# A two-layer hybrid mixer/SwiGLU block: the FFN's opening order, its first down products, and a 4 + 2 split of the last output half

## The chip, the cores and the metric

The kernel runs on one core of one Trainium2 chip. The metric is the device time of one execution in microseconds (us), from the profiler; the engines are TensorE (PE), VectorE (DVE), ScalarE (ACT), GpSimd (POOL) and the queue from which nearly all transfers are issued, SyncE (SP).

## The reference, cut to what matters

Two layers over 512 latent and 256 context tokens of width 1024. A layer is a mixing sub-layer (three head groups, one projection in and one out) and a SwiGLU feed-forward network (FFN), each between two RMS norms with a modulation (shift, scale, gate) that is computed from conditioning vectors. The second layer keeps only the latent tokens after the mixer.

```python
def swiglu(h, w13, w2):              # h: tokens x 1024, FFN_HIDDEN = 2816
    gate, up = jnp.split(h @ w13, 2, axis=-1)
    return (jax.nn.silu(gate) * up) @ w2
...
mod_l = (jax.nn.silu(c) @ ada_w[l] + ada_b[l])[:, None, :]
...
h_l = modulate(rms_norm(lat, norm_ffn_pre[l]), sh2, sc2)
lat = lat + gt2 * rms_norm(swiglu(h_l, ffn_w13[l], ffn_w2[l]), norm_ffn_post[l])
```

Everything is float32.

## The kernel before, in words

**Precision.** A float32 operand of a product is split into a high and a low part of a faster type: ACT casts the high part, DVE or POOL subtracts to get the low part, and three PE products (high-high, high-low, low-high) are summed. So weights cost one ACT cast (`L328`) and one DVE subtraction (`L329`) for each buffer of 128x1024. `wp` holds one raw buffer and four `whi`/`wlo` buffers of this size; `load` and `load13` fill them, and `get(i, ahead=1)` loads one unit ahead in program order.

**Order.** The program is written in one order; a scheduler with a timing model then fixes each engine's order, program order being the priority. Pools are stacks in on-chip memory, on the left and on the right; a tile of a new pool waits for the old tiles that lay where it lies.

**End of the mixer.** For each block of 128 tokens (position `pos`; the order is context blocks 4, 5, then 0 to 3) `out_front` computes the output projection from four units `wos`, two of them in `wp`, two in a right pool; `out_back` of the block before does `post_norm` and `pre_norm`, which ends in PE transposes into `whole` (`L266`, then DVE `L274` and ACT `L272`). Then the rest of the modulation chunks (`ada_some`, products at `L203`) and the FFN.

**FFN up.** A Strassen-Winograd form: `whole` is cut in k (first index) and in token halves (`hn` = 384 columns in layer 0, 256 in layer 1) into b11, b12, b21, b22; DVE makes t1 to t4 from them, and b11, b21, b22, t1 to t4 are split. `thi` and `tlo` take the two buffers of tag `H`; `tlo` lies where `whole` was. For each of 22 hidden blocks f, `ffn_up` takes seven products of 12 matmuls (`prod`, `L1211`): a11 b11, s2 t2, s3 t3, s1 t1, a12 b21, a22 t4, s4 b22. Of the weight combinations POOL makes s3 and s1 (`L367`, `L368`), DVE s2 and s4 (`L369`, `L370`). The hidden block goes to DRAM (`hds`).

**FFN down.** For each half j of the output's 1024 columns, all 2816 hidden rows are read back in pairs of blocks (`hid_pair`: one transfer `hr`, two ACT casts `L1261`, one subtraction on DVE and one on POOL `L1262`) and multiplied with w2 (`down`, `L1270`, 6 matmuls of 512 columns for each pair and position), accumulating one bank for each position: six in layer 0, four in layer 1. w2 comes in groups of 2, 4, 4, 4, 4, 4 blocks. Half 0 is copied to `y0`. In the last group of half 1 the positions end one after another, and `ffn_back` (post-norm, residual, and in layer 0 the pre-norm of layer 1) follows one position behind.

**Pools that matter.** `adp` (constants `cst2` and modulation buffers `araw`, `arow`) lives through the kernel. The FFN's pool `F` (left) is opened after the mixer's pools `rx`, `mx` are closed, and the pool `D` of the down part lies where `F` lay.

Of the kernel before, what the change touches and what calls it, by code (L numbers as in the profile page):

```python
# [11 lines left out]
F32 = mybir.dt.float32  # L12
# [11 lines left out]
NL = 2  # L24
# [59 lines left out]
def tile_backbone(ctx: ExitStack, tc: tile.TileContext, a: dict, out: bass.AP, dbg=None):  # L84
# [274 lines left out]
    def load13(i, srcs):  # L359
        F = state["F"]  # L360
        raw = wtile(wp if i % 2 else F, "raw", [128, 4, 512])
        for dsl, src in srcs:
            DMA.dma_start(raw[:, dsl].rearrange("p s (k n) -> p (s k) n", n=128), src)
        a21, a22, a11, a12 = (raw[:, q] for q in range(4))
        sm = pt(F, "S", [128, 3, 512], bufs=1)
        s2, s3, s4 = (sm[:, q] for q in range(3))
        G.tensor_tensor(s3, a11, a21, ALU.subtract)  # L367
        G.tensor_tensor(a21, a21, a22, ALU.add)  # L368
        V.tensor_tensor(s2, a21, a11, ALU.subtract)  # L369
        V.tensor_tensor(s4, a12, s2, ALU.subtract)  # L370
        t0 = split(wp, raw[:, 2:4], [128, 2, 512], V)
        t1 = split(wp, sm[:, 0:2], [128, 2, 512], V)
        t2 = split(wp, raw[:, 0:2], [128, 2, 512], V)
        t3 = split(wp, sm[:, 2:3], [128, 1, 512], V)
        at = {"a11": (t0, 0), "a12": (t0, 1), "s2": (t1, 0), "s3": (t1, 1), "s1": (t2, 0), "a22": (t2, 1),
              "s4": (t3, 0)}
        return {n: tuple(t[q][:, o].rearrange("p (k n) -> p k n", n=128) for q in range(2))
                for n, (t, o) in at.items()}
# [17 lines left out]
    for l in range(NL):  # L396
# [18 lines left out]

        for f in range(NF):
            u["w13"][f] = add("w13", None,
                              [(slice(0, 2), kblk(w13[:, FF + 128 * f:FF + 128 * f + 128])),
                               (slice(2, 4), kblk(w13[:, 128 * f:128 * f + 128]))])
        for j in range(2):  # L420
            f0 = 0
            for gi, gn in enumerate(GROUPS):
                u["w2"][gi, j] = add("w2", [128, gn, 512],
                                     [((allsl,), kblk(a["ffn_w2"][l, 128 * f0:128 * (f0 + gn),
                                                                  512 * j:512 * j + 512]))])
                f0 += gn
# [65 lines left out]
    adp = ctx.enter_context(tc.tile_pool(name="adp", bufs=2))  # L492
    cst.append(pt(adp, "cst2", [128, CST.shape[1] - NC0], bufs=1))
    S.dma_start(cst[1], a["cst"][:, NC0:])
    ones = C("ones")
    tri = C("tri", "p (a f) -> p a f", a=2)
    gam = C("gam", "p (h f) -> p h f", h=4)
    qgf = C("qgf", "p (r f) -> p r f", r=2)
    qgb = C("qgb", "p (r f) -> p r f", r=2)
    kgf, kgb, rdec, hsel = C("kgf"), C("kgb"), C("rdec"), C("hsel")  # L500
    cosc = C("cos", "p (t f) -> p t f", t=4)
    sinc = C("sin", "p (t f) -> p t f", t=4)

# [6 lines left out]
    for l in range(NL):  # L510
# [6 lines left out]
        tbs_out = [0, 1, 2, 3] if last else tbs_all  # L517
        mx = ctx.enter_context(ExitStack())
# [647 lines left out]
        out_back(*prev)  # L1166
        rx.close()
        mx.close()

        ada_some(adp, len(todo))  # L1170

        hn = tot // 2
        with pool(f"F{l}") as F:
            state["F"] = F
            bhi = pt(F, "bhi", [128, 3, 4, hn], F32R, bufs=1)
            blo = pt(F, "blo", [128, 3, 4, hn], F32R, bufs=1)
            tm = pt(F, "tm", [128, 4, 4, hn], bufs=1)
            thi = pt(hp, "H", [128, 4, 4, hn], F32R)
            b11, b12 = whole[:, 0:4, 0:hn], whole[:, 0:4, hn:tot]
            b21, b22 = whole[:, 4:8, 0:hn], whole[:, 4:8, hn:tot]  # L1180
# [162 lines left out]
```

## Time and profile before

| what | value |
|---|---|
| median of 3 runs | 1896.7 us (1896.48 to 1901.89) |
| the profiled execution, its own time | 1899.01 us |
| its span, first to last instruction | 1897.1 us |
| mean granted TensorE clock | 0.963 of full speed |
| PE busy | 1768.9 us (93%) |
| HBM read, written | 226.82 MB, 36.31 MB |

The profiled execution is one of the same program; 1.9 us of its time lie outside the span. Busy times are sums over instructions; a PE that is busy can run at either of two clocks, 2.4 or 1.2 GHz, and the granted clock of a stretch is given as a share of the higher.

### The profile page before, as it was taken

Reading aid. Unit: us, or ns where it says so; the run is one execution under the profiler, and the core shown is the slowest. Engines: PE = TensorE matmul, PEld = TensorE weight load, DVE = VectorE, ACT = ScalarE, POOL = GpSimd, SP = SyncE. Lnnn points to the kernel's source line nnn. Section 1 sums busy time; section 2 is a strip of 40 time slices with the busy share of each in tenths; the row PEclk is TensorE's granted clock in tenths of the full one; section 3 lists DMA queues with packets and bytes.
Section 4 is the critical chain, followed back from the end, with each engine's and each line's share of the span. In section 5 each row is a group of like instructions: output and inputs, shape, how many; then the busy total and the mean of one; then the engine's idle time right before and its main releaser. Section 6 shows DMA issues by size and latency. Waiting matters only on the chain. (4 is left out here: it accounts for less than half of the span.)

```text
span 1897.1 us, 30528 instructions
## 1 busy us (share of the span) xinstructions
PE 1768.9 (93%) x11915; PEld 1581.0 (83%) x11915; DVE 1172.1 (62%) x2022; ACT 804.7 (42%) x1462; POOL 587.1 (31%) x569
## 2 busy tenths in 40 slices
PE   6999989998969999998999979999998879999898
PEld 4789988877958999998788747998887879999686
DVE  4677688746457565654434357659856488887345
ACT  3546443224553333333323375544334454444333
POOL 1103453204114332331412140145303135555322
PEclk9999999999979999999999989999998979999899
DMA  8334344547432333332645373334434234443753
GB/s 280 118 99 129 109 153 148 158 148 232 151 111 84 109 106 92 92 110 97 246 139 180 112 230 106 95 114 153 143 128 148 78 101 132 126 133 106 281 188 124
DMA packets 261259, 265.10 MB, mean 140 GB/s; under 512 B 13432, under 2 KB 220252, under 8 KB 260988
## 3 DMA queue, kind: packets, MB, share of 16 engines
q1 hardware_dynamic: 260048, 261.86, 43.2%
q8 instruction: 93, 1.52, 0.3%
q10 hardware_dynamic: 1068, 1.31, 0.2%
q14 instruction: 50, 0.41, 0.1%
HBM read 226.82 MB, written 36.31 MB: 139 GB/s over the span
## 5 line engine op out<-in xcount | busy, mean ns | idle before, releaser
L329 DVE TENSOR_TENSOR wlo<-raw,whi 128x1024 fp32r<-128x1024 f32 (+2 forms) x192 | 274.7, 1435 | 163.5 <-ACT whi L328 163.2
L1211 PE MATMUL px<-H,whi 128*128 128x384 f32 (+1 forms) x1408 | 310.9, 312 | 5.7 <-ACT whi L328 5.7
L328 ACT CAST whi<-raw 128x1024 fp32r<-128x1024 f32 (+2 forms) x192 | 194.4, 1018 | 241.1 <-PE px L1211 107.5
L433 PE MATMUL mm<-whi,H 128*128 128x256 f32 x1376 | 269.0, 290 | 7.1 <-ACT stg L793 6.4
L1211 PEld LDWEIGHTS px<-H,whi 128*128 128x128 f32 x1408 | 237.3, 191 | 7.4 <-ACT whi L328 7.4
L433 PEld LDWEIGHTS mm<-whi,H 128*128 128x128 f32 x1376 | 219.4, 192 | 21.8 <-ACT stg L793 9.1
L1211 PE MATMUL px<-H,wlo 128*128 128x384 f32 (+1 forms) x704 | 213.9, 311 | 0.0
L433 PE MATMUL mm<-wlo,H 128*128 128x256 f32 x688 | 198.4, 288 | 0.0
L433 PE MATMUL mm<-H,whi 128*128 128x256 f32 (+2 forms) x720 | 179.6, 338 | 5.5 <-DVE H L490 2.6
L1270 PE MATMUL px<-whi,hidhi 128*128 128x512 f32 x374 | 149.5, 401 | 15.8 <-ACT hidhi L1261 15.8
L1270 PE MATMUL px<-wlo,hidhi 128*128 128x512 f32 x374 | 149.5, 400 | 0.0
L1270 PE MATMUL px<-whi,hidlo 128*128 128x512 f32 x374 | 145.9, 395 | 0.0
L433 PEld LDWEIGHTS mm<-H,whi 128*128 128x128 f32 (+1 forms) x720 | 122.1, 189 | 28.0 <-DVE H L490 3.7
L328 ACT CAST whi<-S 128x1024 fp32r<-128x1024 f32 x88 | 73.6, 836 | 164.3 <-DVE S L369 69.6
L1262 POOL TENSOR_TENSOR hidlo<-hr,hidhi 128x768 fp32r<-128x768 f32 (+1 forms) x44 | 76.6, 1743 | 204.0 <-ACT hidhi L1261 191.5
L433 PEld LDWEIGHTS mm<-wlo,H 128*128 128x128 f32 x688 | 132.4, 192 | 2.4 <-issue 1.3
L1211 PEld LDWEIGHTS px<-H,wlo 128*128 128x128 f32 x704 | 132.4, 191 | 0.0
L1240 POOL TENSOR_TENSOR hf<-hf,g 128x384 f32<-128x384 f32 (+1 forms) x44 | 54.1, 1229 | 241.4 <-issue 174.6
L1211 PE MATMUL mm<-bhi,whi 128*128 128x384 f32 (+1 forms) x352 | 111.2, 316 | 14.2 <-ACT whi L328 14.2
L433 PE MATMUL px<-whi,H 128*128 128x256 f32 x640 | 120.8, 288 | 0.4 <-ACT H L1143 0.4
L433 PE MATMUL mm<-H,wlo 128*128 128x256 f32 (+2 forms) x360 | 120.0, 334 | 0.4 <-DVE wlo L329 0.4
L329 DVE TENSOR_TENSOR wlo<-S,whi 128x1024 fp32r<-128x1024 f32 x88 | 89.2, 1013 | 47.0 <-ACT whi L328 46.8
(304 smaller groups left out, 3920.5 us busy)
## 6 DMA issues: line engine op xcount, KB each, us to landing
araw<-ada_w_dram SPq DMA_DIRECT2D x96, 512.0 KB
raw<-ffn_w_dram SPq DMA_DIRECT2D x92, 512.0 KB
raw<-w_in_dram SPq DMA_DIRECT2D x26, 1024.0 KB
raw<-ffn_w_dram SPq DMA_DIRECT2D x20, 1024.0 KB
hr<-hd SPq DMA_DIRECT2D x22, 768.0 KB
hr<-hd SPq DMA_DIRECT2D x22, 512.0 KB
Rt<-gd SPq DMA_DIRECT2D x40, 256.0 KB
hd<-hf SPq DMA_DIRECT2D x22, 384.0 KB
```

Of the source, the lines that this page charges most:

```text
L328: S.copy(hi, src)
L329: lo_engine.tensor_tensor(lo, src, hi.bitcast(F32), ALU.subtract)
L433: PE.matmul(ps, x(k), y(k), start=(k == 0 and p == 0), stop=(k == n - 1 and p == 2))
L1211: PE.matmul(ps[:, :hn], w[x][:, k], r[y][:, k], start=first and k == 0 and p == 0, stop=k == 3 and p == 2, skip_group_check=True)
L1240: G.tensor_tensor(h1, h1, g1, ALU.mult)
L1262: (G if q else V).tensor_tensor(hh[1][:, q], hr[:, q], hh[0][:, q].bitcast(F32), ALU.subtract)
L1270: PE.matmul(ps, lh[x](k), rh[y](k), start=f + k == 0 and p == 0, stop=f + k == NF - 1 and p == 2, skip_group_check=True)
```

## The change

1. **Opening.** `load13` can load a unit of the gate columns only (`gate_only`: a11 and a12, one split). For the first NA hidden blocks (3 in layer 0, 4 in layer 1) such units are loaded first, and their products a11 b11 and a12 b21 open the FFN; the same blocks' other five products follow in `ffn_up`, whose units fetch all four quarters again but don't split a11 and a12 again (`late`). The splits and combinations of `whole` are made in column blocks of 128 tokens; b21's and b22's low parts and t3 go from DVE to POOL. `bhi`, `blo`, `tm` lie in a right pool `FB`.
2. **Down opening.** At f = 9 the hidden pairs 0 and 2 are read back and split into the place of `tm`; their down products stand ahead of the change from pool `F` to pool `D`.
3. **Passes.** In layer 0 the second column half is done in two passes, four positions and then two, each reading all hidden blocks and its own copy of w2's half. Layer 1 keeps two passes of four.
4. **Pools.** `adp` becomes a pool of each layer, closed before the FFN; layer 1 loads `cst2` again, on ACT's queue. The rest of `ada_some` moves ahead of the pools' closing. The raw buffers of `load13` alternate by f, odd f in `F`.

```diff
-        raw = wtile(wp if i % 2 else F, "raw", [128, 4, 512])
-        for dsl, src in srcs:
-            DMA.dma_start(raw[:, dsl].rearrange("p s (k n) -> p (s k) n", n=128), src)
+        f = srcs["f"]
+        raw = wtile(F if f % 2 else wp, "raw", [128, 4, 512])
+        if srcs["gate_only"]:
+            fetch(2)
+            t0 = split(wp, raw[:, 2:4], [128, 2, 512], V)
+            at = {"a11": (t0, 0), "a12": (t0, 1)}
+        else:
+            fetch(0)
+            fetch(2)
...
+            if not srcs["late"]:
+                t0 = split(wp, raw[:, 2:4], [128, 2, 512], V)
...
+        NA = 3 if l + 1 < NL else 4
+        u["w13a"] = [add13(f, True, False) for f in range(NA)]
...
+        u["passes"] = [(0, range(6)), (1, range(4)), (1, range(4, 6))] if l + 1 < NL else [(0, range(4)), (1, range(4))]
...
+        adp = ax.enter_context(pool(f"adp{l}", 2))
+        cst[1:] = [pt(adp, "cst2", [128, CST.shape[1] - NC0], bufs=1)]
+        S.dma_start(cst[1], a["cst"][:, NC0:])
...
+        ada_some(adp, len(todo))
         rx.close()
         mx.close()
-        ada_some(adp, len(todo))
+        ax.close()
...
+            for i in range(n2):
+                cs = slice(128 * i, 128 * i + 128)
+                rsplit("b11", whole[:, 0:4, cs], cs, V)
+                rsplit("b21", whole[:, 4:8, cs], cs, G)
+            for i in range(n2):
...
+                V.tensor_tensor(t1, b12, b11, ALU.subtract)
+                V.tensor_tensor(t2, b22, t1, ALU.subtract)
+                G.tensor_tensor(t3, b22, b12, ALU.subtract)
+                V.tensor_tensor(t4, b21, t2, ALU.subtract)
+            for i in range(n2):
+                cs = slice(128 * i, 128 * i + 128)
+                for nm, q in (("t2", 1), ("t3", 2), ("t1", 0), ("t4", 3)):
+                    rsplit(nm, tm[:, q, :, cs], cs, V)
+                rsplit("b22", whole[:, 4:8, hn + 128 * i:hn + 128 * i + 128], cs, G)
...
+            for f in range(NA):
+                un = get(u["w13a"][f])
+                ps = [mm(), px()][f % 2]
+                uu = up_first(ps, un)
+                begun[f] = uu, up_gate(ps, un)
             for f in range(NF):
-                ffn_up(f)
+                ffn_up(f, begun.get(f))
+                if f == 9:
+                    he = pt(FB, "tm", [128, 2, 2, 2, tot], F32R, bufs=1)
+                    for i in range(2):
+                        hr = pt(HR, "hr", [128, 2, tot], bufs=2)
+                        hid_load(hr, 2 * i)
+                        early[2 * i] = hid_split(hr, he[:, i, 0], he[:, i, 1])
...
+            first = acc_tiles(0)
+            un = get(u["w2"][0, 0])
+            for pos in range(npos):
+                down(first[pos], early[0], un, 0, pos, 0)
+            un = get(u["w2"][1, 0])
+            for pos in range(npos):
+                down(first[pos], early[2], un, 0, pos, 2)
+        fx.close()
...
+            for pi, (j, poss) in enumerate(u["passes"]):
+                pss = first if pi == 0 else acc_tiles(pi)
+                if pi == 1:
+                    back = begin_back()
...
+                            if prev is not None:
+                                back(*prev)
+                            prev = pos, ps
+                        if prev is not None:
+                            back(*prev)
```

`up_first` is the a11 b11 product with its ACT copy to `uu`, `up_gate` the a12 b21 product into the same bank with its Silu; `begin_back` opens the pool of the backs, loads the gains and returns the old `ffn_back`.

## Rows read from the trace of the kernel before

**Rows 1.** The page, part 1: busy us, share of the span, instructions.

```profile
PE 1768.9 (93%) x11915; PEld 1581.0 (83%) x11915; DVE 1172.1 (62%) x2022; ACT 804.7 (42%) x1462; POOL 587.1 (31%) x569
```

**Rows 2.** Waits of PE, whole span: us in total, times, longest us.

```profile
PE px L1270 <- ACT hidhi L1261: 15.8, 3, 8.2
...
PE mm L1211 <- ACT whi L328: 14.2, 3, 8.4
```

**Rows 3.** Windows: length; PE, PEld, DVE, ACT, POOL busy (instructions); clock, DMA share, GB/s.

```profile
537.20:548.40 11.20, 6.87 (x57) 4.39 (x56) 5.00 (x15) 5.87 (x13) 1.10 (x2) 0.70 0.60 195
548.40:576.50 28.10, 15.64 (x63) 13.76 (x64) 25.58 (x34) 16.80 (x25) 13.20 (x3) 0.75 0.31 91
...
600.00:880.00 280.00, 280.00 (x1613) 280.00 (x1612) 166.09 (x213) 99.44 (x135) 88.00 (x78) 1.00 0.32 95
...
905.00:1000.00 95.00, 95.00 (x409) 76.14 (x408) 39.15 (x27) 33.62 (x43) 31.71 (x15) 1.00 0.53 182
...
1087.10:1130.00 42.90, 27.75 (x203) 17.34 (x202) 25.18 (x49) 31.80 (x67) 19.58 (x26) 0.83 0.71 234
1509.80:1531.00 21.20, 4.61 (x18) 3.92 (x19) 16.38 (x28) 13.83 (x26) 3.96 (x4) 0.61 0.24 75
...
1545.00:1750.00 205.00, 204.43 (x1721) 204.23 (x1720) 168.90 (x227) 95.92 (x144) 112.42 (x82) 1.00 0.43 126
```

**Rows 4.** Timeline of PE, 885 to 910 us: start, length, what.

```profile
900.73 0.79 PE L1270 MATMUL px<-whi,hidhi 128*128 128x512 f32 x1 [8.15 <-ACT hidhi L1261]
...
903.46 0.45 PE L1270 MATMUL px<-whi,hidhi 128*128 128x512 f32 x1
```

**Rows 5.** Timeline of PE, 1750 to 1765 us.

```profile
1762.31 0.80 PE L1270 MATMUL px<-whi,hidhi 128*128 128x512 f32 x1 [7.39 <-ACT hidhi L1261]
```

**Rows 6.** Timeline of ACT, 525 to 592 us.

```profile
537.11 0.60 ACT L243 ACTIVATE y<-px 128x512 f32<-128x512 f32 x1 [3.33 <-PE px L433]
...
551.26 0.80 ACT L272 ACTIVATE H<-px,modc 128x128 f32<-128x128 f32 x2
...
556.14 1.04 ACT L328 CAST whi<-raw 128x1024 fp32r<-128x1024 f32 x1 [2.62 <-DMA raw<-ffn_w_dram]
```

**Rows 7.** Timeline of DVE, 525 to 592 us.

```profile
562.79 0.69 DVE L369 TENSOR_TENSOR S<-raw 128x512 f32<-128x512 f32 x1 [2.52 <-POOL raw L368]
...
567.75 1.22 DVE L329 TENSOR_TENSOR wlo<-raw,whi 128x1024 fp32r<-128x1024 f32 x1
...
569.48 7.03 DVE L1190 TENSOR_TENSOR H<-tm,H 128x768 fp32r<-128x768 f32 x8
```

**Rows 8.** Timeline of POOL, 525 to 592 us.

```profile
556.33 5.08 POOL L367 TENSOR_TENSOR S<-raw 128x512 f32<-128x512 f32 x1 [12.54 <-DMA raw<-ffn_w_dram]
...
569.64 9.15 POOL L367 TENSOR_TENSOR S<-raw 128x512 f32<-128x512 f32 x1 [6.89 <-DVE wlo L329]
...
590.19 1.30 POOL L367 TENSOR_TENSOR S<-raw 128x512 f32<-128x512 f32 x1 [1.76 <-DVE wlo L329]
```

**Rows 9.** Lines by form, 892.6 to 1087 us: busy us, mean ns of one | idle before.

```profile
L1262 POOL TENSOR_TENSOR hidlo<-hr,hidhi 128x768 fp32r<-128x768 f32 x22 | 43.4, 1976 | 119.0 <-ACT hidhi L1261 106.9 <-DVE hidlo L1262 6.5 <-PE pa L1270 5.6
...
L1261 ACT CAST hidhi<-hr 128x768 fp32r<-128x768 f32 x44 | 34.5, 832 | 76.6 <-issue 35.7 <-PE pa L1270 15.8 <-DMA hr<-hd 14.1
...
L1262 DVE TENSOR_TENSOR hidlo<-hr,hidhi 128x768 fp32r<-128x768 f32 x22 | 24.2, 1102 | 58.7 <-ACT hidhi L1261 58.7
```

**Rows 10.** Transfers, 900 to 1087 us: packets, MB, rate; share of 16 engines.

```profile
DMA packets 15000, 32.01 MB, mean 171 GB/s; under 512 B 2720, under 2 KB 3744, under 8 KB 14990
...
q1 hardware_dynamic: 14990, 31.88, 50.0%
```

**Rows 11.** Lines by form, 1073 to 1130 us (the six backs of layer 0).

```profile
L278 POOL TENSOR_TENSOR H<-hh,H 128x512 fp32r<-128x512 f32 x12 | 15.7, 1324 | 16.4 <-ACT H L277 16.4
...
L297 DVE TENSOR_TENSOR x<-x,y 128x1024 f32<-128x1024 f32 x6 | 8.2, 1368 | 1.6 <-DMA x<-xsd 1.5
```

More of the change, by code (lines that the diff above doesn't have):

```diff
@@ L1173, in tile_backbone @@
+        early = {}
+        fx = ctx.enter_context(ExitStack())
+        HR = fx.enter_context(pool(f"HR{l}", side="right"))
+        FB = fx.enter_context(pool(f"FB{l}", side="right"))
         with pool(f"F{l}") as F:
             state["F"] = F
-            bhi = pt(F, "bhi", [128, 3, 4, hn], F32R, bufs=1)
-            blo = pt(F, "blo", [128, 3, 4, hn], F32R, bufs=1)
-            tm = pt(F, "tm", [128, 4, 4, hn], bufs=1)
+            bhi = pt(FB, "bhi", [128, 3, 4, hn], F32R, bufs=1)
+            blo = pt(FB, "blo", [128, 3, 4, hn], F32R, bufs=1)
+            tm = pt(FB, "tm", [128, 4, 4, hn], bufs=1)
@@ new lines, in tile_backbone, with rsplit @@
+            rhs = {"b11": (bhi[:, 0], blo[:, 0]), "b21": (bhi[:, 1], blo[:, 1]), "b22": (bhi[:, 2], blo[:, 2])}
+            rhs |= {f"t{q + 1}": (thi[:, q], tlo[:, q]) for q in range(4)}
+            def rsplit(nm, src, cs, eng):
+                hi, lo = (x[:, :, cs] for x in rhs[nm])
+                S.copy(hi, src)
+                eng.tensor_tensor(lo, src, hi.bitcast(F32), ALU.subtract)
+            for i in range(n2):
+                cs = slice(128 * i, 128 * i + 128)
+                rsplit("b11", whole[:, 0:4, cs], cs, V)
+                rsplit("b21", whole[:, 4:8, cs], cs, G)
@@ new lines, in tile_backbone, with hid_pair, begin_back, ffn_back @@
+            for pos in range(npos):
[4 more added lines that the diff above has]
+        fx.close()
+        with pool(f"D{l}") as Dp:
+            y0 = pt(Dp, "y0", [128, npos, 512], bufs=1)
+            def hid_pair(f):
+                hr = pt(Dp, "hr", [128, 2, tot], bufs=2)
+                hid_load(hr, f)
+                return hid_split(hr, *(pt(Dp, t, [128, 2, tot], F32R, bufs=3) for t in ("hidhi", "hidlo")))
+            dx = ctx.enter_context(ExitStack())
+            back = {}
+            def begin_back():
+                nf = dx.enter_context(pool(f"nf{l}", 2))
+                gw = load_gw(Dp, nf, l, 1, [0] if last else [0, 1])
+                if last:
+                    xs = [x_tile(nf, xsd[128 * tb:128 * tb + 128, :], 4) for tb in tbs_out]
+                else:
+                    H["t"], H["f"] = hpair()
+                def ffn_back(pos, ps):
+                    tb = tbs_out[pos]
+                    tsl = slice(128 * tb, 128 * tb + 128)
+                    dst = out[0, tsl, :] if last else xsd[tsl, :]
+                    cut = last and pos == npos - 1
+                    x = xs[pos] if last else x_tile(nf, xsd[tsl, :])
+                    x = post_norm(nf, [y0[:, pos], ps], x, gw[:, 0 if tb < 4 else 1], dst, cut)
+                    if not last:
+                        pre_norm(nf, l + 1, 0, tb, x)
+                return ffn_back
+            for pi, (j, poss) in enumerate(u["passes"]):
+                pss = first if pi == 0 else acc_tiles(pi)
+                if pi == 1:
+                    back = begin_back()
```

211 lines of the change are left out of this document (93 added, 118 removed).

## The prediction

> **What bounds the kernel now.** I read the page's busy shares first: PE is busy 93% of the span, the next engine 62% [rows 1]. Then windows by stage: in the FFN's up stretches and in the down stretch PE is busy all the time (280.0 of 280, 204.4 of 205, 95 of 95 us at clock 1.00) [rows 3]. So PE binds, and a change can gain only where PE idles or runs at its lower clock. PE's list of waits names the two places that this change touches: 15.8 us for the first cast of the hidden rows (two long ones, one in each layer), and 14.2 us for the first weight casts of the FFN [rows 2]. The windows show how poor the stretches around them are: 537.2 to 576.5 has PE busy 22.5 of 39.3 us at clock 0.70 to 0.75, 1509.8 to 1531 only 4.6 of 21.2 at 0.61, and the end of layer 0's FFN (1087.1 to 1130) 27.75 of 42.9 at 0.83 [rows 3].
>
> To price an opening I put the steady pace against its end. Layer 0: 280/1613 = 0.1736 us a matmul, 22 x 84 = 1848 of them make 320.8 us [rows 3]; the last ends at 900.73 - 8.15 = 892.6 [rows 4], so the stage behaves as if it began at 571.8. Layer 1: 205/1721 = 0.1191, 220.1 us [rows 3], ending 1762.31 - 7.39 = 1754.9 [rows 5], so 1534.8. The mixer's last projection in layer 0 ends at 537.1 [rows 6], 34.7 us ahead of that start.
>
> **Opening.** The edit moves 3 x 24 matmuls (12.5 us) of layer 0, and 4 x 24 (11.4 us) of layer 1, into the gap. PE work is not added. How much of the gap closes depends on when the other products can start, and that is a sum over DVE and POOL. Between 548.4 and 576.5 DVE is busy 25.6 of 28.1 us [rows 3]; the POOL instruction that takes 1.30 us alone took 5.08 and 9.15, the longer one while DVE ran eight low-part subtractions in a row (7.03 us) [rows 7, 8]. DVE's 25.6 and two POOL instructions of 1.3 make 28.2: the stretch itself. So I add two-input work of both engines as if one at a time.
>
> The Trainium skill speaks against moving work to POOL here: SBUF — State Buffer, section "Who interferes with whom", says that a DVE instruction with two SBUF inputs and a POOL instruction that reads SBUF take turns at one port pair, each for its whole length. The trace agrees that they do not run side by side (9.15 us for 1.30), but POOL got no turn between DVE's instructions. By the rule taken literally a POOL instruction would wait for one DVE instruction (1.22 us at most here) and take 2.5 us, and my sum would be the same, as it counts both engines' work once.
>
> Layer 0 in units from [rows 7, 8], a DVE instruction over 512 columns 0.69, a 1024-column split 1.22, POOL 1.30: b11 low 3 x 0.69; two residual adds 2.4; t1, t2, t4 9 x 0.69; twelve low parts 8.3; block 0's s2, s4 and three splits 4.5; POOL's nine moved pieces 11.7 and s3, s1 2.6. Sum 37.8, of which 4.0 come after what s2 t2 needs. Starting at 537.1 (the right pool's old tiles, the last `wos`, are then free), s2 t2 can start at 570.9; block 1's units need 7.1 us more, 0.7 beyond block 0's 10.4 us on PE. Equivalent start 570.9 + 0.7 - 12.5 = 559.1 against 571.8: gain 12.7, taken as 13. Bounds: 0 if the sum grows by 13 us, and 24 if POOL hides under DVE, when the chain from the last position (results at 551.26 + 0.80 = 552.1 [rows 6], three combinations, nine low parts at 0.69) gives 560.4.
>
> Layer 1, same way with two column blocks: 1.4 + 1.4 + 4.1 + 5.5 + 4.5 + 2.4 (gate splits that come late) + 7.8 + 2.6 = 29.7, less 4.0, from 1509.8: 1535.5. Blocks 0 to 3 then give PE only 60 x 0.1191 = 7.1 us each where DVE is busy 168.9 and POOL 112.4 of 205 us, 8.2 and 5.5 us a block [rows 3]; without the gate split (1.22) I allow 1 us of lag a block, an estimate. 1535.5 + 4 - 11.4 = 1528.1 against 1534.8: gain 7, bounds 0 and 16.
>
> `tlo` lies on `whole`, whose last readers are now POOL's t3 and b22. So DVE's twelve low parts, and behind them on DVE the weight splits that PE waits for, queue on POOL. The last column's pieces can be done some 2.1 + 2.6 us after 552.1, well inside the sum, so no term of its own. The seven extra fetches of 512 KB on SP cost nothing: transfers are at share 0.31 in that stretch [rows 3]; without that cover each is 0.52 MB at 91/0.31 = 294 GB/s, 1.8 us.
>
> **First down products.** They remove the waits of 8.15 and 7.39 us, and the lower clock behind them: seven matmuls between 900.73 and 903.46 take 2.7 us where 95/409 = 0.232 us each gives 1.6 [rows 3, 4, 5]. That is 17.7 us. In their place 72 and 48 matmuls (16.7 and 11.1 us) cover the next pair's transfer and first cast (the same 8.2 and 7.4 us), its second cast (0.83) and POOL's half (1.98) [rows 9]: 11.0 and 10.2 us. Layer 1 is tight. w2's first group must be split by then; its raw buffer is freed a block earlier than before, since block 21 now uses `F`. I take 16; bounds 8 (one layer still waits) and 17.7. The two early pairs' splits fall into the up stage: free in layer 0 (DVE 166 of 280 us), but in layer 1 DVE and POOL have little room, 4 us of work, charged 2; bounds 0 and 4.
>
> **The 4 + 2 split.** PE's work is the same. The third pass reads 22 blocks of hidden rows and of w2 again, 22 x 0.655 = 14.4 MB, and splits them again, for 11 x 12 x 0.232 = 30.7 us of PE. A pair takes 2.8 us of PE; on ACT 2 x 0.83 + 1.04 = 2.7; on DVE and POOL together 1.22 + 1.10 + 1.98 = 4.3 [rows 6, 7, 9]. The transfers ran 171 GB/s at half share, so 342 GB/s full, 3.8 us a pair [rows 10]. All but PE need more than before, and four backs fall into the same time: 2 x 1.32 on POOL and 1.37 on DVE each [rows 11], and about 6.4 us on ACT (31.8 us for five of them [rows 3], an estimate). From the end of the first position, 8.4 us before the third pass: 47.3 + 16.0 less 4.3 prefetched = 59 us for DVE and POOL, so the pass lasts 50.6 us; ACT gives 52.6 and so 44; transfers 42 and less what is prefetched. I take 50.6, 20 more than PE's.
>
> What it buys: only two of six backs follow the last matmul. After it I allow 16 us, the mixer's last back from 537.1 to 552.1 [rows 6] and a cast. In 8.4 + 50.6 + 16 = 75.0 us PE does 8.4 + 30.7 of down products, 48 transposes (6.2), 72 matmuls of the next layer's first unit (8.6) and one modulation chunk (1.6): 55.5, a loss of 19.5, with some 2.5 for the lower clock 22. Before, the same stretch lost 15.2 idle and about 4 at the lower clock [rows 3]. Net -3. Bounds: +17 if the pass runs at PE's pace, and the slow rival below. The modulation chunks that partly filled the old tail move to layer 1's mixer; they are work on either side of this count. `cst2` on ACT's queue waits for `y0`'s last reader; ACT's pre-norm casts stand behind it. That reader comes early in the last back, so 0; if the order is unlucky, up to 5.
>
> **Sum.** 13 + 7 + 16 - 2 - 3 = 31 from the profiled execution's 1899.0 (span 1897.1 and 1.9 around it): 1868. The median is 2.3 below that execution, so 1866.
>
> **Rivals.**
> Everything hides (12%): transfers and splits run far enough ahead for the third pass to keep PE's pace. Speaks for it: DVE is busy 39 and POOL 32 of 95 us in the down stretch [rows 3], so there is room earlier; against: three hidden buffers hold only three pairs. 20 us better: 1846.
> The openings give nothing (13%): POOL starves behind DVE as in [rows 8], `tlo` comes late, and PE waits with its gate products done. The skill's rule on the port pair, above, is this rival's mechanism; the trace bears it out for single instructions. 20 us worse: 1886.
> The third pass costs more (15%): casts, subtractions and backs follow one another instead of overlapping, 65 us instead of 50.6: 1881.
> Slower than before (10%): the third pass waits for transfers. With the backs' 4.2 MB it moves 18.6 MB; at 342 GB/s that is 54 us, mostly hidden, but the down stretch as a whole moved 171 GB/s [rows 10]. At 200 GB/s it takes 93 us, 42 more: 1908. It decides from 84 us on, below about 221 GB/s. Against it: the old tail ran 234 GB/s at share 0.71 [rows 3].
> My forecast holds the other 50%, with its own range 1852 to 1878.
>
> **How the numbers follow.** The range 1847 to 1888 leaves out about half of the best case, the slow one and a tail of the second, 2 in 10. About 0.3% (5.7 us) is what a measurement can tell from no change. The forecast, the best case and most of the second and third lie below 1891: faster 0.85; their tails 0.06 the same; the slow rival less its tail 0.09.
>
> **What would show it.** Right: PE's waits for `hidhi` at the two FFN turns under 2 us; gate products of `bhi` from about 541 and 1514; s2 t2 near 571 and 1535; down products starting near 880 in layer 0; a third pass of 45 to 55 us whose PE waits name ACT's or POOL's hidden splits; about 15 us from the last down product to the last transposes. Wrong: s2 t2 later than 584 in layer 0; PE waits on `hr` transfers through the whole third pass; new waits of layer 1's scans for `cst2`, or layer 1's modulation chunks holding up its output projection.

## The result, and the profile after

The changed kernel takes 1913.0 us (median of 8, 1905.1 to 1917.4) against 1896.6 (1893.8 to 1902.6): ratio 1.0081, 95% interval 1.006 to 1.0102. It is slower by 0.8%; the prediction was 1866, with a range of 1847 to 1888. The profiled execution took 1915.99 us, span 1914.0. Page of the changed kernel, part 1, against [rows 1]:

```profile
PE 1777.2 (93%) x11915; PEld 1590.8 (83%) x11915; DVE 1200.0 (63%) x2041; ACT 828.9 (43%) x1501; POOL 634.9 (33%) x595
```

PE has the same instructions and idles 136.8 us instead of 128.2. Where that time went is read from five marks on PE's lines: the last product of each mixer's output projection, the end of each up part (the first down product where that follows at once), and the last down product of layer 0. They stand at 536.8, 892.6, 1087.1, 1508.6 and 1754.9 us before and at 536.4, 891.3, 1121.4, 1535.3 and 1783.2 after. Lengths between them in us:

| stretch | before | after | gain |
|---|---|---|---|
| start to the end of layer 0's mixer | 536.8 | 536.4 | 0.4 |
| layer 0, mixer to the end of up | 355.8 | 354.9 | 0.9 |
| layer 0, end of up to the last down product | 194.5 | 230.1 | -35.6 |
| from there to the end of layer 1's mixer | 421.5 | 413.9 | 7.6 |
| layer 1, mixer to the end of up | 246.3 | 247.9 | -1.6 |
| layer 1, end of up to the end | 142.2 | 130.8 | 11.4 |

Only the last row is near what was foreseen: layer 1's turn has no wait any more (7.39 us in [rows 5]). Its mark is not the same in both kernels: after the change the first down products of layer 1 stand ahead of the last 12 up products; PE's timeline there:

```profile
1783.20 0.39 PE L1328 MATMUL pa<-whi,tm 128*128 128x512 f32 x1
...
1786.61 0.28 PE L1250 MATMUL px<-bhi,wlo 128*128 128x256 f32 x1
```

These 12 are 1.4 us of work (0.119 us each) that the table counts in the last row, so with the products counted alike layer 1's up part lost 3.0 us and the last stretch gained 12.8. In the kernels below with fewer than four gate units in layer 1, 24 up products (2.9 us) stand behind the mark.

Windows of the changed kernel around layer 0's down part (length; PE, PEld, DVE, ACT, POOL busy; clock, DMA share, GB/s), against [rows 3]:

```profile
891.30:908.25 16.95, 16.95 (x73) 13.32 (x72) 5.28 (x5) 4.53 (x5) 1.02 (x1) 1.00 0.41 139
908.25:920.00 11.75, 5.70 (x14) 4.47 (x14) 3.75 (x3) 4.18 (x5) 4.92 (x3) 0.72 1.04 398
920.00:1050.00 130.00, 130.00 (x574) 107.64 (x573) 55.25 (x45) 49.83 (x65) 43.43 (x22) 1.00 0.57 196
1050.00:1081.00 31.00, 13.84 (x58) 10.81 (x57) 21.03 (x33) 25.55 (x51) 17.15 (x15) 0.72 0.70 248
1081.00:1122.00 41.00, 31.71 (x114) 23.18 (x113) 22.10 (x21) 23.92 (x33) 20.73 (x12) 0.83 0.62 199
1122.00:1152.00 30.00, 18.24 (x115) 12.88 (x114) 12.86 (x22) 16.05 (x32) 7.72 (x15) 0.66 0.65 217
```

The early products run without a gap for 17 us, but then PE stops. The third pass, from 1050.5 to 1121.8, takes 71 us where PE has 30.7 us of products: two parts, of which the first has PE busy 13.8 of 31 us. PE's waits from 1052 to 1124 us name the backs' normalized rows `xn`, then w2's casts and low parts (us in total, times, longest):

```profile
PE px L266 <- ACT xn L257: 11.1, 3, 5.1
PE pa L1328 <- ACT whi L328: 7.7, 4, 3.5
PE pa L1328 <- DVE wlo L329: 5.8, 3, 4.8
```

ACT's timeline shows why (start, length, what):

```profile
1055.28 1.56 ACT L1204 CAST hidhi<-hr 128x768 fp32r<-128x768 f32 x2
1056.75 1.04 ACT L328 CAST whi<-raw 128x1024 fp32r<-128x1024 f32 x1
1057.98 1.06 ACT L243 ACTIVATE y<-x 128x1024 f32<-128x1024 f32 x1 [0.19 <-DVE x L297]
...
1063.37 1.15 ACT L257 ACTIVATE xn<-x,rs 128x1024 f32<-128x1024 f32 x1 [2.36 <-POOL rs L250]
...
1080.86 0.46 ACT L272 ACTIVATE hh<-px,modc 128x128 f32<-128x128 f32 x1 [0.85 <-DVE hh L274]
1081.22 1.04 ACT L328 CAST whi<-raw 128x1024 fp32r<-128x1024 f32 x1
```

From 1057.8 to 1081.2 ACT holds the backs of the second pass and not one cast of w2 or of hidden rows. The openings, PE's timeline of the changed kernel:

```profile
549.69 0.69 PE L1250 MATMUL mm<-bhi,whi 128*128 128x384 f32 x1 [2.08 <-ACT bhi L1224]
557.12 0.69 PE L1250 MATMUL mm<-blo,whi 128*128 128x384 f32 x1 [6.74 <-DVE blo L1225]
576.58 2.29 PE L1250 MATMUL px<-H,whi 128*128 128x384 f32 x6 [4.74 <-ACT whi L328]
...
914.30 0.80 PE L1328 MATMUL pa<-whi,hidhi 128*128 128x512 f32 x1 [6.05 <-ACT hidhi L1204]
```

Gate products start at 549.7 instead of 541 and stop at once for `blo`; s2 t2 comes at 576.6 instead of 570.9, and waits for its weights; at layer 0's turn the wait of 8.15 us [rows 4] is 6.05. In layer 1 s2 t2 starts 33.5 us after the mixer (1568.8), before it was 23.4 (1532.0).

### The profile page after: what moved, and what is told of

Read it like the earlier page. It is cut to its first block, busy times and chain, and to the rows that moved or that the text cites. A ratio compares the mean times of both kernels' runs of the same rounds, so it can differ in the third digit from the quotient of the medians.

```text
span 1914.0 us, 30680 instructions
## 1 busy us (share of the span) xinstructions
PE 1777.2 (93%) x11915; PEld 1590.8 (83%) x11915; DVE 1200.0 (63%) x2041; ACT 828.9 (43%) x1501; POOL 634.9 (33%) x595
## 5 line engine op out<-in xcount | busy, mean ns | idle before, releaser
L328 ACT CAST whi<-raw 128x1024 fp32r<-128x1024 f32 (+2 forms) x204 | 205.2, 1016 | 239.1 <-PE px L1250 87.7
L453 PE MATMUL mm<-whi,H 128*128 128x256 f32 x1376 | 273.0, 292 | 12.9 <-ACT stg L813 10.4
L453 PEld LDWEIGHTS mm<-whi,H 128*128 128x128 f32 x1376 | 222.1, 195 | 28.4 <-ACT stg L813 13.3
L1205 POOL TENSOR_TENSOR hidlo<-hr,hidhi 128x768 fp32r<-128x768 f32 (+1 forms) x51 | 95.4, 1873 | 188.8 <-ACT hidhi L1204 174.0
L1250 PE MATMUL mm<-blo,whi 128*128 128x384 f32 (+1 forms) x328 | 103.7, 316 | 9.0 <-DVE blo L1225 9.0
L1250 PE MATMUL mm<-bhi,whi 128*128 128x384 f32 (+1 forms) x328 | 104.3, 318 | 4.5 <-ACT bhi L1224 3.5
L453 PEld LDWEIGHTS px<-whi,H 128*128 128x128 f32 x640 | 101.7, 193 | 5.3 <-issue 2.0
L1250 PE MATMUL mm<-bhi,wlo 128*128 128x384 f32 (+1 forms) x328 | 103.6, 316 | 0.9 <-DVE wlo L329 0.9
```

Of the source, the lines that this page charges most:

```text
L328: S.copy(hi, src)
L453: PE.matmul(ps, x(k), y(k), start=(k == 0 and p == 0), stop=(k == n - 1 and p == 2))
L1205: (G if q else V).tensor_tensor(lo[:, q], hr[:, q], hi[:, q].bitcast(F32), ALU.subtract)
L1250: PE.matmul(ps[:, :hn], w[x][:, k], r[y][:, k], start=first and k == 0 and p == 0, stop=k == 3 and p == 2, skip_group_check=True)
```

## The experiments

Unless something else is said, each is the changed kernel with the edit shown; ratios are to the kernel before. "Six" is the first edit below. Times are medians, stage lengths come from one profiled execution of each kernel. Eleven kernels with the changed kernel's openings differ by 2.5 us in layer 0's up part (352.6 to 355.1) and by 1.5 in layer 1's.

**1. One pass of six in layer 0.**

```diff
-        u["passes"] = [(0, range(6)), (1, range(4)), (1, range(4, 6))] if l + 1 < NL else ...
+        u["passes"] = [(0, range(6)), (1, range(6))] if l + 1 < NL else ...
-                    return [mm(), mm(), px(), px()]
+                    return [mm(), mm()] + [px() for _ in range(npos - 2)]
```

> The changed kernel, with layer 0's second half as one pass of six positions again; openings, first down products and pools stay as changed. My theory: the third pass is what made the change slower. In the changed kernel layer 0's down stretch ends 36 us later relative to its up stage, and the tail behind it (to the steady projections) is 16 us shorter; with one pass of six both go back, so 1913 - 20 = 1893 (1888 to 1898), and the stretch from the last up product to the last down product falls from 230.5 to about 192 us. Rival: the pools cost it (modulation chunks and constants that moved into layer 1's mixer): then the third pass was about even as I predicted (-3) and this kernel stays at 1905 to 1916.

1887.0 us, 0.9941 [0.9917, 0.9964]: 26 us below the changed kernel and faster than before. The stretch from the end of up to the last down product falls to 188.9 us, from there to the end of layer 1's mixer it takes 425.6: together 614.5, against 644.0 after and 616.0 before. The split in three passes is the loss. Of the some 10 us that six gains over the kernel before, about 6 are products that run in less time than before, which no term of the prediction has (last section).

**2 to 6. What the third pass waits for.** Narrow columns, backs between the pairs, both, both with a second raw buffer, and the second raw buffer alone:

```diff
 # narrow: in pass 2 a pair is read and split for two positions only
+                n = slice(128 * u["passes"][pi][1][0], tot) if pi == 2 else slice(0, tot)
+                hid_load(hr, f, n)          # hview[:, f:f + 2, n]
 # inter: backs of pass 1 go between the pairs of pass 2
+                            if pending and (f + k0) % 4 == 2:
+                                back(*pending.pop(0))
 # raw2: w2's groups alternate between two raw buffers in the down part
+        raw = wtile(state["D"] if name == "w2" and state.get("D") and i % 2 else wp, "raw", shape)
```

> The third pass reads and splits only the columns of its two positions (256 of 768), so that its transfers, casts and subtractions of hidden rows fall to a third; the backs stand where they stood. Theory Q (order in the queues): what holds the pass first is that ACT's queue holds the four backs of the second pass ahead of the splits, 23 us from 1058.0 to 1081.2 without one cast of a hidden row or of w2; that stays, and only the 41 us behind it shrink, towards PE's pace: third pass 66 to about 55, 1903 (1899 to 1908). Theory V (volume): the pass is slow because each pair costs three times the transfer and split that two positions need; then it comes down to about 40 us and the time to 1887 (1883 to 1892).

> The backs of the second pass's four positions are put between the pairs of the third pass (one after every second pair) instead of ahead of them; hidden rows are read at full width as before. Theory Q: the first casts of the third pass follow the second pass at once, PE's 23 us with little work go, the pass is then held by transfers and splits, 66 to 50 us: 1897 (1893 to 1902). Theory V: the sum of the work on ACT, DVE, POOL and the queues is the same, so it moves at most 4 us: 1909 to 1913.

> Both edits. Theory Q with the rest at PE's pace: the third pass falls from 66 us to 36 to 42 (30.7 of products and 6 of transposes), 1913 - 27 = 1886 (1882 to 1891). Theory V: as the narrow kernel alone, within 4 us of it.

> The narrow and interleaved kernel, with a second raw buffer for w2 in the down part's pool (groups alternate). Theory R (one raw buffer): with both edits before, the fetches of w2's groups still followed one another at 10.4, 9.6, 11.2 and 8.5 us, since a group's transfer waits until the subtraction of the last one has read the single raw buffer, then come transfer, two casts, two subtractions; PE needs 5.6 us a group of four blocks for two positions. With a second buffer the transfer runs beside the splits; the stretch from the last product of the second pass in bank mm to the last down product falls from 58.0 to 46 to 50 us: 1881 (1878 to 1885). Rival: PE's own queue sets it, transposes of the backs standing in it ahead of products and waiting for the normalized rows: then nothing moves, 1887 to 1892.

> The changed kernel with only the second raw buffer for w2; backs ahead of the third pass, hidden rows at full width. Theory Q: ACT's queue keeps the third pass from its first splits as before, and then casts of full width stand beside it; the 41 us behind fall by some 5 (ACT needs 2.7 us a pair, DVE and POOL together 4.3): 1908 (1904 to 1912). If the single buffer is all that holds the pass, it comes near PE's pace at once: 1893 or below.

| kernel | us | ratio | third pass, us |
|---|---|---|---|
| changed | 1913.0 | 1.0081 [1.006, 1.0102] | 71 |
| narrow | 1903.4 | 1.0022 [1.0007, 1.0037] | 62 |
| inter | 1908.0 | 1.0046 [1.0028, 1.0065] | 69 |
| both | 1890.4 | 0.9961 [0.9945, 0.9976] | 52 |
| both, second raw buffer | 1885.0 | 0.994 [0.9917, 0.9964] | 39 |
| second raw buffer alone | 1915.5 | 1.0098 [1.008, 1.0116] | 69 |

The third pass is taken from its first to its last product on PE's line. Narrow came out where theory Q had it. Inter alone came out near V's end (1909), not in Q's range, so order by itself is not the cause; but both together gain 22.6 us, 8 more than the sum of the two, and the second buffer alone gives nothing (1908 was expected). So neither theory holds alone: each obstacle hides the next. PE's waits in inter's third pass show it; those for the backs fell from 11.1 us to 1.9, those for w2 rose from 13.5 to 19.6:

```profile
PE pa L1328 <- ACT whi L328: 11.5, 5, 3.9
PE pa L1328 <- DVE wlo L329: 8.1, 4, 4.0
PE px L266 <- ACT xn L257: 1.9, 1, 1.9
```

With both edits the next was the raw buffer; SP's timeline, fetches of w2's groups in "both":

```profile
1057.31 0.38 SPq L342 DMA_DIRECT2D raw<-ffn_w_dram  x1
1067.75 0.38 SPq L342 DMA_DIRECT2D raw<-ffn_w_dram  x1
1077.33 0.37 SPq L342 DMA_DIRECT2D raw<-ffn_w_dram  x1
1088.54 0.37 SPq L342 DMA_DIRECT2D raw<-ffn_w_dram  x1
```

That is one group of four blocks every 10 us, where PE needs 5.6. The second buffer brought the pass to 39 us, PE's products and transposes (30.7 + 6.2), but the time fell by 5 only. PE's waits from 1040 to 1130 us of that kernel name what comes next (us in total, times, longest):

```profile
PE pa L203 <- DMA araw<-ada_w_dram: 8.9, 1, 8.9
PE pa L1328 <- ACT hidhi L1204: 3.0, 1, 3.0
```

The first is a wait for modulation weights in the tail, which the changed kernel has too (6.35 us at 1139.7).

**7. Layer 0's turn.** Six, with the first hidden pairs ahead of the next weight group in program order; then with their transfers on POOL's queue; then with those of pairs 4 and 6 read in the up part:

```diff
 # 7a
-            un = get(u["w2"][1, 0])
+            un = get(u["w2"][1, 0], 0)
+                    pre = {k0: hid_pair(f + k0) for k0 in ks}   # pass 0, third group, ahead of its get
 # 7b, instead
+                hid_load(hr, f, G if pi == 0 and f in (4, 6) else DMA)
 # 7c, instead
+                if f == 15:
+                    for f2 in (4, 6):
+                        ahead[f2] = pt(HR, "hr", [128, 2, tot], bufs=2)
+                        hid_load(ahead[f2], f2)
```

> One pass of six, and at the turn from up to down the transfers of the first two pairs read in the down part stand ahead of the third weight group in program order. Theory S (SP's queue): layer 0's wait of 6.2 us for the first cast comes from SP, which holds the hidden rows' transfer behind a weight transfer that waits 9.05 us for the raw buffer; with the order turned round the wait falls under 1 us and the lower clock behind it goes: 1887 - 6 = 1881 (1878 to 1884). Rival: the wait moves to the weights of that group, which now come later: 1885 to 1888.

> One pass of six, and the transfers of the first two hidden pairs of the down part are issued by POOL's queue, so that SP's order no longer matters (in the last try at this the order on SP stayed as it was: the weight transfer first, 8.96 us of waiting, then the hidden rows). Theory S: layer 0's wait of 6 us for the first cast after the early products goes, and the lower clock behind it: 1887 - 6 = 1881 (1879 to 1883). Rival: the weights of the next group, which come 9 us after their own wait, hold PE next: 1885 to 1888.

> One pass of six, and the hidden rows of pairs 4 and 6 are read during the up part (behind block 15) into the buffers of the early pairs, so that at the turn neither their transfer nor the order on SP matters, and the casts on ACT stand ahead of the fourth weight group's. When POOL's queue issued these transfers they landed at 900, 6.3 us after their issue, but the cast came at 913.5, behind two weight casts that wait 8.4 and 6.8 us for w2 through the one raw buffer. Theory O (ACT's order behind the raw buffer): now the cast can come at about 904, the products of the early pairs last until 906 to 908, the wait of 6 us and the lower clock behind it go: 1887 - 6 = 1881 (1878 to 1883). Rival: the third weight group itself is late, and PE stops at pair 6: 1885 to 1889.

7a: 1885.1, the wait stays (6.2 us), and SP's order too: the scheduler kept the weights first. 7b: 1889.4, wait 6.4 us. Theory S falls: the rows landed 5.7 to 6.8 us after their issue, by about 900, and ACT did not get to them. POOL's and ACT's timelines of 7b:

```profile
893.33 1.63 POOL L1200 DMA_DIRECT2D hr<-hd  x2
...
903.78 2.00 ACT L328 CAST whi<-raw 128x1024 fp32r<-128x1024 f32 x2 [8.37 <-DMA raw<-ffn_w_dram]
912.55 1.04 ACT L328 CAST whi<-raw 128x1024 fp32r<-128x1024 f32 x1 [6.76 <-DMA raw<-ffn_w_dram]
913.50 3.03 ACT L1204 CAST hidhi<-hr 128x768 fp32r<-128x768 f32 x4
```

7c: 1872.4, 0.9885 [0.9855, 0.9916]. ACT's timeline now:

```profile
898.18 2.00 ACT L328 CAST whi<-raw 128x1024 fp32r<-128x1024 f32 x2 [6.64 <-DMA raw<-ffn_w_dram]
900.09 3.03 ACT L1204 CAST hidhi<-hr 128x768 fp32r<-128x768 f32 x4
907.50 1.05 ACT L328 CAST whi<-raw 128x1024 fp32r<-128x1024 f32 x1 [4.39 <-DMA raw<-ffn_w_dram]
```

The casts precede the cast that waits for the raw buffer, PE goes on at 904.0 without a wait, and the down stretch takes 180.3 instead of 188.9 us: 8.6. Theory O holds for the mechanism; the time is lower than its 1878 to 1883. The profiled execution is the fastest of the four (1868.5 to 1878.5) and 18.3 us below that of six; 6.6 of these lie in layer 1's mixer (419.0 instead of 425.6), which this edit doesn't touch. The other kernels with six have 421.7 to 426.3 us there, 424.0 in a later one with the same edit; the rest is not explained.

**8. The openings.** Six, with a raw buffer of its own for gate units of even blocks; the same with b21's, b22's low parts and t3 back on DVE; six without gate units; with them in layer 0 only; with three and two:

```diff
 # 8a own buffer
+        if srcs["gate_only"] and f % 2 == 0:
+            raw = pt(F, "rawg", [128, 1024], bufs=1).rearrange("p (s n) -> p s n", n=512)
 # 8b and DVE
-                rsplit("b21", whole[:, 4:8, cs], cs, G)
+                rsplit("b21", whole[:, 4:8, cs], cs, V)
 # 8c, 8d, 8e
-        NA = 3 if l + 1 < NL else 4
+        NA = 0                                # 8d: 3 and 0, 8e: 3 and 2
```

> One pass of six, and the gate units of even hidden blocks get a raw buffer of their own (4 KB a partition), so that the first full unit's fetch no longer waits for the last gate unit's split. Theory W (weights late): in the changed kernel s2 t2 waited 4.7 us in layer 0 and, at a time when the token side was ready for 8 us, in layer 1 for its weight cast behind this fetch; both go, s2 t2 starts near 572 in layer 0 and 7 us earlier after the mixer in layer 1: 1887 - 9 = 1878 (1875 to 1882). Rival: the sum over DVE and POOL holds the opening, as the prediction counted it; earlier weights then only stand in the same queue: 1884 to 1888.

> As the kernel with own buffers for the gate units (1885.7), and b21's and b22's low parts and t3 back on DVE. If the two engines' two-input work adds up as the prediction summed it (one at a time), the change of engine costs nothing: 1883 to 1889. If POOL's nine pieces ran beside DVE, DVE gets 9 x 0.69 us more in layer 0 and 6 x 0.69 in layer 1: 10 us slower, 1893 to 1898.

> One pass of six, and no gate units (NA = 0 in both layers): the blocks are computed as before, with splits and combinations still in column blocks and partly on POOL. It prices the gate products. From the stages: layer 0's mixer end to the last up product takes 353.4 us with them and 355.5 before, layer 1's 249.1 against 245.1; so I expect the openings to be worth next to nothing: 1883 to 1890. Rival (the prediction's term): they fill 12.5 and 11.4 us of idle PE, and something else in the opening gives it back; then this kernel is 12 to 20 us slower, 1899 to 1907.

> One pass of six; gate units in layer 0 only (NA = 3 and 0). With no gate units at all layer 0's up stage was 6.2 us longer and layer 1's 7.4 us shorter (359.6 and 241.7 us from the mixer's end to the last up product, against 353.4 and 249.1). If these two are independent: 1887 - 7 = 1880 (1877 to 1883). Rival: the 7.4 us come from the state of clock and queues that layer 0 hands on: 1885 to 1889.

> One pass of six; three gate units in layer 0, two in layer 1. Theory K (lower clock): layer 1's 96 gate products run at clock 0.5 to 0.6 and take about 28 us instead of the 11.4 of the prediction; s2 t2 stands behind them and starts 33.5 us after the mixer, 21.3 without them. With 48 of them it starts at about 25 and nothing of the gap is lost: 1879 to 1882. Rival (lag): each gate unit costs later, since blocks without gate products need less of PE than of DVE: half of the 7 us comes back, 1883 to 1885.

| kernel | us | layer 0, mixer to end of up | layer 1, same | layer 1, end of up to the end |
|---|---|---|---|---|
| six | 1887.0 | 353.4 | 249.4 | 131.9 |
| 8a own buffer | 1885.7 | 351.4 | 250.2 | 131.3 |
| 8b own buffer, DVE | 1878.2 | 348.8 | 252.2 | 131.5 |
| 8c no gate units | 1889.5 | 359.6 | 242.0 | 138.1 |
| 8d in layer 0 only | 1890.0 | 353.7 | 246.9 | 140.2 |
| 8e three and two | 1889.2 | 354.9 | 246.9 | 138.3 |

8a: s2 t2 of layer 0 comes 5.6 us earlier behind the mixer (34.6 against 40.2), but the up part is only 2.0 us shorter: theory W explains the wait it named, not the opening. Behind s2 t2 PE has gate products left, and DVE works without a pause from 546 to 578. The test is not clean either: the own buffer lies in the up part's pool and opens late, so the first gate product starts 19.2 us behind layer 0's mixer instead of 13.3, and 16.5 instead of 2.6 behind layer 1's, where s2 t2 comes 1.6 us earlier and not 7. 8b: with the pieces that the change moved to POOL back on DVE, layer 0's up part is 2.6 us shorter and layer 1's 2.0 longer; its executions fell in two groups (1886.6 and 1888.0; 1875.5, 1876.4 and 1878.2), and the profiled one is of the longer group, so the total decides little. 8c prices layer 0's gate products at 6.2 us, half of the 12.5 that they hold. In layer 1 the kernels without four gate units shorten the up part by 1.1 to 6.0 us (the products behind the mark counted alike), but then PE waits at layer 1's turn again (5.4 us for `hidhi` in 8d) and the rest is 5 to 7 us longer. 8d missed its 1880: layer 1's code is that of 8c, and its up part gained 1.1 us, not 6.0. So these totals don't decide between theory K and the lag.

**9. A guess that fell: the modulation chunks.** In the tail before, 88 of the 256 products at L203 run; in six 32, and 112 instead of 48 in the late mixer.

```diff
-        adp = ax.enter_context(pool(f"adp{l}", 2))
+        adp = ax.enter_context(pool(f"adp{l}", 2, "right"))
```

> One pass of six, and the layer's modulation pool on the right side of on-chip memory, where layer 0's tokens parts were (free since the down part began), instead of over the down part's buffers. Theory C (chunks): before, 88 of the 256 modulation products of the stretch ran in the tail of layer 0's FFN, where PE idles, and 48 in the late mixer; now 32 and 112, since their buffers become free only with the down part's. That is 8 us of PE work put where PE is busy, and the mixer is 7 us longer than before. With buffers free early the products go back into the tail: 1887 - 7 = 1880 (1877 to 1883). Rival: the order of the program, not the memory, puts them late: 1885 to 1888.

The counts went back to 88, 40, 80 and 48, and the time stayed, 1886.5 against 1887.0. Where the chunks run costs nothing here; the prediction's treatment of them stands.

**10. Together.** Six with 7c, 8b and gate units in layer 0 only; the same with layer 1's four; and the first with the third pass of experiment 5 in place of six:

> One pass of six, rows of pairs 4 and 6 read ahead, gate units in layer 0 alone and with own raw buffers, b21's, b22's low parts and t3 on DVE. Sum of the single edits as measured or expected: 1887 - 6 (turn) - 7 (no gate units in layer 1) - 3 (own buffers, DVE) = 1871 (1867 to 1877). Rival: the edits win the same time (waits that follow one another): 1877 to 1882.

> As the best kernel so far (1867.0), but with layer 1's four gate units as in the change. From layer 1's mixer end to the end of the program it took 376.1 us without gate units; the other kernels with one pass of six and four gate units took 380 to 383, those without or with two 380 to 387, where a wait at layer 1's turn stood against the gain. With that wait gone in both: if layer 1's gate products cost time of their own, 1869 to 1873; if they give what the prediction counted (7 us), 1858 to 1862; if they are worth nothing, 1865 to 1869.

> The best kernel so far with the 4 + 2 split in place of the pass of six, with its three obstacles removed (backs between the pairs, two positions' columns only, a second raw buffer). Without the other edits the split with these came to 1885.0 against 1887.0 for the pass of six: nothing. So 1862 to 1870, the same within the measurement. Rival (the split is worth its -3 or more once PE does not wait): below 1862. Rival (its tail waits for the modulation weights, 11.5 us in the last such kernel, and this grows): above 1871.

| kernel | us | ratio | layer 1, mixer to end of up, and to the end |
|---|---|---|---|
| all, six | 1867.0 | 0.9845 [0.9822, 0.9868] | 244.4, 132.0 |
| all, six, layer 1's gate units | 1876.8 | 0.9892 [0.9876, 0.9909] | 251.7, 131.7 |
| all, three passes | 1864.8 | 0.9834 [0.9819, 0.9849] | 243.3, 135.7 |

The sum of the single edits came out (1871 expected), but not by its terms: measured singly the turn had given 14.6 us instead of 6, the missing gate units of layer 1 had cost 3 instead of giving 7, and own buffers with DVE had given 8.8 instead of 3. Two versions beat the kernel before by 29 and 33 us. With the wait at the turn gone in both, layer 1's gate units cost 10 us by the medians; between the two profiled executions it is 7.3, of which 5.9 lie in the up part, the products behind the mark counted alike. PE's timeline of layer 1's opening with them:

```profile
1502.26 1.97 PE L266 MATMUL px<-cst,xn 128*128 128x128 f32 x8 [9.38 <-ACT xn L257]
1509.07 0.58 PE L1255 MATMUL mm<-bhi,whi 128*128 128x256 f32 x1 [4.85 <-ACT whi L328]
...
1523.30 0.74 PE L1255 MATMUL px<-H,whi 128*128 128x256 f32 x4 [0.44 <-ACT whi L328]
```

and without:

```profile
1494.00 0.38 PE L1255 MATMUL mm<-bhi,whi 128*128 128x256 f32 x1 [1.45 <-ACT bhi L1229]
1495.49 0.58 PE L1255 MATMUL mm<-blo,whi 128*128 128x256 f32 x1 [1.11 <-DVE blo L1230]
...
1514.14 1.44 PE L1255 MATMUL px<-H,whi 128*128 128x256 f32 x5 [5.41 <-ACT H L1229]
```

Without gate units the first full unit lies split in `wp` when the mixer ends, and its products start 2.6 us behind the last projection (1491.4). With them the first gate unit's buffer, here its own in the up part's pool, opens only then, and the products start 17.4 us behind (1491.7 to 1509.1). The granted clock is 0.62 up to s2 t2 (1491.7 to 1523.3), without gate units 0.81 (1491.4 to 1514.1). The changed kernel has this first unit in `wp` and starts at 2.6 us too; what is shown is the cost of the four units in this form. For the form of the changed kernel the nearest pair is 7c against "all, six", about 2 us of the up part with the products counted alike, within what these readings scatter. Whether it is the lower clock or the late weights stays open.

The three passes, freed, equal six within the measurement (1864.1 to 1869.2 against 1863.9 to 1869.6).

## Why the prediction was wrong

The largest error is the third pass, taken at 50.6 us, which lasted 71. The openings and layer 0's turn gave little of what was counted.

**What bounds it, and first down products (16 predicted).** PE does bind. Layer 1's turn gave what was counted: its last stretch is 12.8 us shorter, of which the wait is 7.39, the clock behind it about 1.3 (six matmuls, not seven, lie between 900.73 and 903.46, so each turn lost 1.3 us and not 1.1), and the shorter down products 3.2 (last section). In layer 0 some 2 us came of 9.2. The step that failed: "72 and 48 matmuls (16.7 and 11.1 us) cover the next pair's transfer and first cast". In layer 0 the cover was as long as counted (17 us), and transfer and cast as short (6.3 us in 7b, 0.8 us). But SP issued the transfer only at 906.35, behind a transfer of w2 that waited for the single raw buffer, and on ACT the cast stood until 912 behind casts of w2 that wait for the same buffer. 7b takes away the first and gains nothing; 7c, which gets the rows in ahead and so the cast too, gave 8.6 us.

**The 4 + 2 split (-3 predicted, about -26 measured by experiment 1).** The step that failed is the length of the third pass: 50.6 us as the largest of three sums (DVE and POOL 50.6, ACT 44, transfers 42), as if they ran side by side. The pass took 71. ACT first did 23 us of backs without a split; then each group of w2 went through transfer, casts and subtractions one behind the other in a single buffer. Removing these and the full-width splits brought it to 39 us. Even so the split gains nothing over six (1885.0 against 1887.0, and 1864.8 against 1867.0). The rival of 65 us named the mechanism ("follow one another instead of overlapping") and was given 15%. The slow rival had the place and nearly the time (1908), not the cause as far as the runs show it: the rate was 199 to 248 GB/s, near its 221, but the transfer engines were busy 0.62 to 0.70 of the time, and PE's and ACT's waits name backs and the raw buffer; narrow transfers with narrow splits left 62 us, and transfers were not tried by themselves. The tail took 31 us to steady products at about 1152, not 16, with 6.35 of them a wait for modulation weights.

**Opening of layer 0 (13 predicted, 0.9 measured).** The sum of DVE and POOL was about right, though it has one residual add of 1.2 us too many (one falls behind 537.1, at 540.5): the low parts of t were done at 572.3, and 8b agrees that moving pieces to POOL buys nothing. The Trainium skill, SBUF — State Buffer, section "Who interferes with whom", has a rule for this: DVE instructions with two inputs in on-chip memory and POOL instructions that read there share a port pair, which is an exclusive lock. The trace agrees: POOL needed 8.23 us for five pieces of 1.30, and in that time DVE's pieces of 0.69 took 1.37 to 1.75. So here POOL did get turns between DVE's instructions, other than in [rows 8]. What failed is "s2 t2 can start at 570.9". The gate products were done at 571.8, as counted, but the weights were late: the full unit's raw buffer is held by the third gate unit, whose low part waits in DVE's queue until 561.4; the fetch lands at 570, POOL's s3 and s1 follow at 570.0 to 574.7, s2 t2 at 576.6, at half clock until 582. "The seven extra fetches of 512 KB on SP cost nothing" priced their bytes, not the buffer. Counted back from its end at the steady pace, as the prediction did, the stage now behaves as if it began at 568.0 instead of 571.8, a gain of 3.8 and not 12.7: s2 t2 takes 5.7 us of the difference, the half clock 2.5. Slower products with `bhi` (last section) then take some 2 us back. 8a removes the wait and wins 2.0 us; the first gate products are later there, and DVE is late with `blo` and with their weights.

**Opening of layer 1 (7, less 2 for the early splits; -3.0 measured).** "1535.5 + 4 - 11.4" counts the four gate products as done, at full speed, by the time s2 t2 is ready. The gap to s2 t2 grew from 23.4 to 33.5 us, with the clock at 0.74 in it: PE was busy 20.9 of the 33.5 and the token side ready at 1560. The experiments with no or two gate units in layer 1 have 245 to 250 us against 249 to 254, the products behind the mark counted alike, so what the four units cost is not settled.

**Chances.** 9% for slower, all on one rival. The other rivals were priced singly and each left the time at 1886 or below; what came was several of them at once. The prediction's own prices for two of them, 20 us for the openings and 15 for the third pass, already make 1901 together. The terms shared a cause, queues behind a single raw buffer.

## What to carry to other kernels

A pass that is shortened for PE must be priced by the chain through its single buffer and by what stands ahead in each engine's queue; the largest of the engines' busy sums is only its floor. When PE work is moved ahead of a wait, follow the first late operand through every queue: here it was late three times (opening, turn, third pass) in a queue that led back to one raw buffer. And remove obstacles together before judging an idea: each of three edits to the third pass gained 10 us or less, and together they turned 71 us into 39.

## What was not expected of the hardware

The same matmuls took different times after their operands had moved in on-chip memory. Lines of the product in layer 0's up part, 650 to 880 us, before (min, median, max in ns):

```profile
L1211 PE MATMUL px<-H,whi x499: 333/334/346, 650.0 to 879.9; 128*128 128x384 f32 x167
L1211 PE MATMUL mm<-bhi,whi x128: 332/336/336, 652.6 to 879.4; 128*128 128x384 f32 x128
```

and after, with `bhi` in another pool and `H` in its old place:

```profile
L1250 PE MATMUL px<-H,whi x494: 334/334/338, 652.0 to 879.9; 128*128 128x384 f32 x165
L1250 PE MATMUL mm<-bhi,whi x128: 337/340/342, 649.9 to 878.2; 128*128 128x384 f32 x128
```

That is 4 ns more for each product with `bhi`; 36 of 84 in a block read `bhi` or `blo`, and the blocks follow at 14.69 instead of 14.60 us, 2 us over the 22. The down products went the other way, 394 to 389 ns. In the changed kernel both lengths stand side by side in layer 1, 395 ns for hidden rows that lie where `tm` was and 389 for the others:

```profile
L1328 PE MATMUL px<-whi,hidhi x98: 389/389/397, 1796.3 to 1904.3; 128*128 128x512 f32 x98
...
L1328 PE MATMUL px<-whi,tm x24: 392/395/402, 1783.4 to 1795.6; 128*128 128x512 f32 x24
```

From start to start a down product takes 226.7 instead of 233.3 ns (over stretches of 12), which over the 1200 outside the early pairs makes 8 us, 6 net of the up part's 2. All the later kernels have the same two paces, so none of them tells what the plan alone is worth without this. Why the place matters was not tried.
